# The opening of a two-layer diffusion block: modulation by eighths, products by k tile, written out in order

## The chip, the cores and the metric

One core of a Trainium2 chip runs the whole program. The metric is device microseconds of one execution. TensorE multiplies, ScalarE (ACT) and VectorE (DVE) do the rest, GpSimd (POOL) takes small powers, SyncE (SP) issues nearly all DMA.

## What is computed

Two layers of a hybrid block on 256 latent tokens and 256 context tokens of 1024 channels. Each layer modulates its norms with shifts, gains and gates that come from a condition vector through a large matrix:

```python
m = (silu(c) @ w_ada + b_ada).reshape(1, 1, 9, 1024)        # and mc, from c_ctx
def pre(t, mm, i, gi):  return rms_norm(t, g[gi]) * (1 + mm[:, :, i + 1]) + mm[:, :, i]
def post(t, y, mm, i, gi, wres):  return t + wres * mm[:, :, i + 2] * rms_norm(y, g[gi])
h = post(h, swiglu(pre(h, m, 0, 0), ffn_wi[0], ffn_wo[0]), m, 0, 1, 0.5)   # and hc, with mc
# then attention, a windowed attention, a short convolution; then a second swiglu
def swiglu(u, wi, wo):  g, up = split(u @ wi, 2);  return (silu(g) * up) @ wo
```

All data are float32. The first thing that needs TensorE at length is the first `u @ wi`: 512 tokens, 1024 channels in 8 k tiles, 2816 hidden columns in 22 column tiles, with a gate half and an up half each.

## The kernel before, in words

Token tiles of 128 tokens are H[0] to H[3] (0, 1 latent, 2, 3 context). A float32 product is done as three products of a rounded format: each operand is split into a rounded upper half (ScalarE casts, line 93 for weights into `w[:, 0]`, line 263 for activations into `Uh`) and a remainder (VectorE subtracts, lines 94 and 264, `w[:, 1]` and `Ul`). For one column tile f, one half u and one k tile, three matmuls of 128x512 go into one PSUM bank: upper weight by `Uh`, upper weight by `Ul`, remainder weight by `Uh` (lines 305 to 307). A column tile has 48 of them.

The opening is `pre_first` (line 246) and the first `up_all([0, 1, 2], "k")` of `ffn`. `pre_first` takes the token tiles in the order 2, 3, 0, 1: `normed_t` (line 217) squares both halves on ScalarE, POOL takes the power -1/2, ScalarE scales the tile into `xn`, TensorE turns it by 8 transposes, and ScalarE copies the result to `XT` (line 251). Then come four quarters of the modulation, `ada_quarter` (line 126): 2 MB of `w_ada` in four loads (tiles `adas`), 32 float32 matmuls with the condition as 32-column weights `S`, four of them side by side (line 135), a copy to `grow` (line 138), a transpose (line 140), and VectorE makes the shift `COLS` and the gain `GP` (lines 118 and 122) for two k tiles. `uf` is `XT` scaled and shifted (line 261), and is split into `Uh` and `Ul`. With mode "k", the products of column tiles 0, 1 and 2 go quarter by quarter, two k tiles at a time, in six PSUM banks of the tags `at`, `mm` and `pv`.

Loads go through one queue on SP, in program order. `stg` has two buffers, and a weight load waits until the earlier weight in its buffer is split. The order of the instructions on each engine is set by a scheduler that simulates the program; the kernel's text gives priorities and dependencies. The modulation of all later parts is done on VectorE between other work (`ada_step`, line 147) and is not touched.

## Time and profile before

| | us |
|---|---|
| median of 3 runs | 1709.74 |
| lowest, highest | 1707.21, 1710.19 |
| profiled execution | 1709.25 |
| its span, first to last instruction | 1707.5 |
| TensorE busy in the span | 1677.3 (98%) |
| VectorE, ScalarE, POOL busy | 1148.4, 720.0, 51.1 |
| granted clock, mean | 0.996 |

The time of an execution is its span and a little around it, here 1.75 us. A busy TensorE in the profile is not one at its peak, since the ends of matmuls are modelled; the start of one matmul after the next is the better measure. A granted clock of 1.00 is 2.4 GHz, 0.50 is 1.2 GHz.

### The profile page before, as it was taken

To read this page: it belongs to the slowest core of one execution; us is meant where nothing else is said; L and a number is where in the kernel's file an instruction comes from. 1 tells how busy PE (TensorE), PEld (TensorE's weight loads), DVE (VectorE), ACT (ScalarE), POOL (GpSimd) and SP (SyncE) were. 2 spreads that over 40 slices of the span, in tenths; PEclk is the share of its full clock that TensorE was granted. 3 is DMA by queue.
4 is the path that set the end of the run, shared out by engine and by line. 5 is a ranking of instruction groups with operands and counts; after the bars stand their busy time and mean duration, and the time that the engine had idled before them with its cause. 6 is when DMAs were issued, how large, how long until landed. Compare 5 with 4: busy or idle time off the path is not lost.

```text
span 1707.5 us, 23320 instructions
## 1 busy us (share of the span) xinstructions
PE 1677.3 (98%) x9012; PEld 1412.0 (83%) x9012; DVE 1148.4 (67%) x1915; ACT 720.0 (42%) x1246; POOL 51.1 (3%) x76
## 2 busy tenths in 40 slices
PE   6999999999999999999999999999999999989997
PEld 4888888888877788888888888888888888779997
DVE  3578788667766665475676557778775768766654
ACT  5432222227656583322222364322222657765442
POOL 1000000002000010000000010000000110000000
PEclk9999999999999999999999999999999999999999
DMA  8566555423121234454444235665563323346551
GB/s 316 206 226 200 172 196 197 161 87 112 62 81 43 93 124 160 148 198 150 156 162 136 75 123 186 209 197 197 172 197 113 114 78 118 118 162 219 176 196 63
DMA packets 75567, 260.38 MB, mean 152 GB/s; under 512 B 10536, under 2 KB 13824, under 8 KB 74560
## 3 DMA queue, kind: packets, MB, share of 16 engines
q1 hardware_dynamic: 74256, 253.34, 44.1%
q0 software_dynamic: 1200, 5.55, 0.9%
q8 instruction: 71, 1.16, 0.3%
q14 instruction: 40, 0.33, 0.1%
HBM read 257.76 MB, written 1.09 MB: 152 GB/s over the span
## 4 chain that ended last, share of the span: by engine, by line
PE 96%; DMA 1%; DVE 1%; ACT 1%; issue 0%; SPq 0%; DVEq 0%; POOLq 0%; ACTq 0%
PE mm L79 51%; PE at L79 27%; PE pv L79 15%; PE ptr L581 2%; PE ptr L225 1%; DMA GT<-in_qkg_dram 1%; ACT junk L208 0%; DVE w L94 0%; DMA H<-in_xin_dram 0%; DMA stg<-in_wi_tm_dram 0%; DVE H L271 0%; PE ptr L462 0%; PE ptr L377 0%; ACT xn L220 0%; ACT XT L251 0%
## 5 line engine op out<-in xcount | busy, mean ns | idle before, releaser
L79 PE MATMUL mm<-Uh,w 128*128 128x512 f32 (+1 forms) x1808 | 486.7, 348 | 0.0
L93 ACT CAST w<-stg 128x1024 fp32r<-128x1024 f32 x262 | 274.5, 1050 | 440.4 <-PE mm L79 396.7
L94 DVE TENSOR_TENSOR w<-stg,w 128x1024 fp32r<-128x1024 f32 x262 | 319.7, 1222 | 164.6 <-ACT w L93 163.9
L79 PEld LDWEIGHTS mm<-Uh,w 128*128 128x128 f32 x1808 | 318.7, 189 | 43.5 <-issue 1.9
L79 PE MATMUL mm<-Ul,w 128*128 128x512 f32 (+1 forms) x904 | 314.9, 348 | 0.0
L162 DVE CUSTOM_DVE_ANT_0 uf<-adas,CB 128x1024 f32<-128x1024 f32 x248 | 302.9, 1221 | 17.6 <-DMA adas<-in_w_ada_dram 13.6
L79 PE MATMUL at<-Uh,w 128*128 128x512 f32 (+1 forms) x960 | 253.9, 344 | 0.3 <-ACT Uh L263 0.3
L79 PE MATMUL mm<-w,a 128*128 128x512 f32 x924 | 226.7, 389 | 0.0
L79 PEld LDWEIGHTS mm<-w,a 128*128 128x128 f32 x924 | 173.4, 188 | 35.8
L79 PEld LDWEIGHTS mm<-Ul,w 128*128 128x128 f32 x904 | 171.1, 189 | 21.5 <-issue 0.5
L79 PEld LDWEIGHTS at<-Uh,w 128*128 128x128 f32 x960 | 168.9, 190 | 22.2 <-ACT Uh L263 0.5
L79 PE MATMUL mm<-w,Uh 128*128 128x512 f32 (+1 forms) x544 | 171.8, 388 | 0.0
L79 PE MATMUL at<-Ul,w 128*128 128x512 f32 (+1 forms) x480 | 165.4, 344 | 1.0 <-DVE Ul L264 1.0
L79 PE MATMUL at<-w,a 128*128 128x512 f32 x594 | 146.7, 390 | 0.1
L79 PEld LDWEIGHTS at<-w,a 128*128 128x128 f32 x594 | 111.0, 188 | 23.4 <-ACT a L316 1.0
L79 PE MATMUL pv<-Uh,w 128*128 128x512 f32 (+1 forms) x464 | 127.7, 353 | 0.0
L79 PEld LDWEIGHTS mm<-w,Uh 128*128 128x128 f32 x544 | 100.4, 188 | 19.8 <-issue 0.7
L311 DVE TENSOR_TENSOR sg<-mm,sg 128x512 f32<-128x512 f32 (+1 forms) x86 | 51.3, 597 | 89.5 <-PE mm L79 83.5
L94 DVE TENSOR_TENSOR w<-stgx,w 128x1024 fp32r<-128x1024 f32 x58 | 71.0, 1224 | 53.1 <-ACT w L93 52.9
L79 PE MATMUL mm<-w,Ul 128*128 128x512 f32 (+1 forms) x272 | 105.3, 387 | 0.8 <-DVE Ul L244 0.8
L79 PEld LDWEIGHTS at<-Ul,w 128*128 128x128 f32 x480 | 91.2, 190 | 12.5 <-DVE Ul L264 1.6
L79 PEld LDWEIGHTS pv<-Uh,w 128*128 128x128 f32 x464 | 82.7, 189 | 12.0
(159 smaller groups left out, 1734.3 us busy)
## 6 DMA issues: line engine op xcount, KB each, us to landing
adas<-in_w_ada_dram SPq DMA_DIRECT2D x144, 512.0 KB, 3.7
stg<-in_wi_dram SPq DMA_DIRECT2D x124, 512.0 KB, 4.2
stg<-in_wo_dram SPq DMA_DIRECT2D x66, 512.0 KB, 3.3
stg<-in_win_dram SPq DMA_DIRECT2D x40, 512.0 KB, 3.3
stgx<-in_wi_dram SPq DMA_DIRECT2D x36, 512.0 KB, 4.3
stgx<-in_wo_dram SPq DMA_DIRECT2D x22, 512.0 KB, 4.2
stg<-in_woa_dram SPq DMA_DIRECT2D x16, 512.0 KB, 3.3
stg<-in_wi_tm_dram SPq DMA_DIRECT2D x16, 512.0 KB, 3.4
```

What stands on the lines that cost most here:

```text
L79: pe.matmul(out, lhsT=lhsT, rhs=rhs, start=first, stop=last)
L93: act.copy(w[:, 0], s)
L94: dve.tensor_tensor(out=w[:, 1], in0=s, in1=w[:, 0].bitcast(F32), op=ALU.subtract)
L162: dve.tensor_tensor_reduce(out=junk, in0=s, in1=CB[:, v], op0=ALU.mult, op1=ALU.add, scale=1.0, scalar=0.0, accum_out=ada_mc[m][:, v, cb:c ...
L225: pe.transpose(pt[:, b], xn[:, 128 * k:128 * k + 128], I)
L311: dve.tensor_tensor(out=sg[:, 0:n], in0=pss[f, 1][:, 0:n], in1=sg[:, 0:n], op=ALU.mult)
L581: pe.transpose(pt[:, b], P[:, 128 * b:128 * b + 128], I)
```

## The change

The function `ada_quarter` goes, and `pre_first` is rewritten. It now also loads the weights of the first three column tiles, splits them, does their products and gives back the six filled banks, and `ffn` takes them as `first`. `in_order` chains all instructions traced under it, on each engine, in the order in which they are written, in place of the scheduler's.

The modulation comes in eighths, one k tile each: two loads of 512 KB (`load_ada`), 16 matmuls (`ada_mm`), a copy to `R`, and one matmul of `R` by a small selection matrix `SELM` (`ada_sel`), which replaces the transpose and adds the two halves of the sum. The layout of `w_ada0` in memory follows. The weights of column tiles 0, 1 and 2 are loaded between the first eighths (`load_w`), tile 1 into two buffers of its own.

Token tiles are no longer scaled and transposed: the rsqrt is put on a diagonal (`diag`), and `flip` multiplies the tile by it. Half of the squares and half of the copies go to VectorE (`square`, `keep`). `unit` makes one k tile of `Uh` and `Ul`, the latent half on ScalarE, the context half on VectorE. Ahead of all this TensorE does 16 products of a constant tile (`spin`).

```diff
+    cur, last_of = {}, {}
+
+    @contextmanager
+    def in_order():
+        traced = nc.cur_bb.bb.instructions
+        n0 = len(traced)
+        yield
+        last_of.clear()
+        for ins in traced[n0:]:
+            if ins.engine in last_of:
+                tc.add_manual_dep(ins, last_of[ins.engine].name,
+                                  mybir.DependencyInfo(mybir.DependencyClass.NoSync, mybir.DependencyReason.DATA),
+                                  reason="traced order")
+            last_of[ins.engine] = ins
...
-    def ada_quarter(ph, qd):
...
 
     def pre_first(ph):
         U = new_u()
+        WU = ph.tile([128, 512], F32R, name="WU", tag="WU")
+        dve.memset(WU.bitcast(F32), 1.0)
         XT = ph.tile([128, 8, 512], F32, name="XT", tag="XT")
...
+        SELM = ph.tile([128, 2, 2], F32, name="SELM", tag="SELM")
+        for m in range(2):
+            dve.tensor_reduce(out=SELM[:, m], in_=I[:, 64 * m:64 * m + 64].rearrange("p (q r) -> p r q", q=2)[:, 0:2],
+                              op=ALU.add, axis=AX.X)
+        dummy = ps_tr.tile([128, 4, 128], F32, name="ptr", tag="ptr").rearrange("p b c -> p (b c)")
+
+        def spin(n):
+            for _ in range(n):
+                mm(dummy, WU[:, 0:128], WU, True, True)
+
+        pts, rs, dgs = {}, {}, {}
+
+        def square(t):
+            s0 = sumsq(H[t][:, 0:512], 512)
+            s1 = small.tile([128, 1], F32, name="s1", tag="s1")
+            sq = ph.tile([128, 512], F32, name="sq", tag="sq")
+            dve.tensor_tensor_reduce(out=sq, in0=H[t][:, 512:1024], in1=H[t][:, 512:1024], op0=ALU.mult, op1=ALU.add,
+                                     scale=1.0, scalar=0.0, accum_out=s1)
+            rs[t] = rsum(sum_eps(s0, s1))
+
+        def diag(t):
+            dgs[t] = ph.tile([128, 128], F32, name="dg", tag="dg", bufs=2)
+            act.activation(dgs[t], I, AF.Copy, scale=rs[t])
+
+        def flip(t, hbs=(0, 1)):
+            for hb in hbs:
+                pt = cur["mm"]().rearrange("p (b c) -> p b c", b=4)
+                for b in range(4):
+                    k = 4 * hb + b
+                    mm(pt[:, b], H[t][:, 128 * k:128 * k + 128], dgs[t], True, True)
+                pts[t, hb] = pt
+
+        def keep(t, hb):
+            xt = XT[:, 4 * hb:4 * hb + 4, 128 * t:128 * t + 128]
+            if hb == 0:
+                act.copy(xt, pts[t, 0])
+            else:
+                dve.tensor_copy(out=xt, in_=pts[t, 1])
+
+        psa, ws, pss, Rs = {}, {}, {}, {}
+
+        def load_ada(j):
+            psa[j] = []
+            for h in range(2):
+                s = ph.tile([128, 4, 2, 128], F32, name="adas", tag="adas", bufs=6)
+                sp.dma_start(out=s.rearrange("p a b c -> p (a b c)"), in_=w_ada0[j, h])
+                psa[j].append(s)
+
+        def ada_mm(j):
+            p = ps_tr.tile([128, 4, 128], F32, name="ptr", tag="ptr")[:, 0]
+            ss = psa.pop(j)
+            for kt in range(8):
+                for m in range(2):
+                    g = 2 * m + kt % 2
+                    mm(p[32 * g:32 * g + 32], S[:, kt], ss[kt // 4][:, kt % 4, m], kt < 2, kt >= 6)
+            R = ph.tile([128, 128], F32, name="R", tag="R", bufs=2)
+            act.copy(R, p)
+            Rs[j] = R
+
+        def ada_sel(j):
+            pt = ps_tr.tile([128, 4, 128], F32, name="ptr", tag="ptr")
+            mm(pt[:, 0, 0:4], Rs.pop(j), SELM.rearrange("p m v -> p (m v)"), True, True)
+            for m in range(2):
+                set_cols(m, j, 1, pt[:, 0, 2 * m:2 * m + 2].unsqueeze(1))
+
+        def unit(j):
+            tag = "uf" if j % 2 == 0 else "xn"
+            uf = work.tile([128, 1024], F32, name=tag, tag=tag)
+            for v in range(2):
+                c = slice(256 * v, 256 * v + 256)
+                g, sh = GP[0][:, j, v:v + 1], COLS[0][:, j, v:v + 1]
+                if v == 0:
+                    act.activation(uf[:, c], XT[:, j, c], AF.Identity, scale=g, bias=sh)
+                else:
+                    dve.tensor_scalar(out=uf[:, c], in0=XT[:, j, c], scalar1=g, scalar2=sh, op0=ALU.mult, op1=ALU.add)
+            act.copy(U[0][:, j], uf[:, 0:512])
+            dve.tensor_tensor(out=U[1][:, j], in0=uf[:, 0:512], in1=U[0][:, j].bitcast(F32), op=ALU.subtract)
+
+        stage = {}
+
+        def load_w(f):
+            for u in range(2):
+                if f == 1:
+                    stage[f, u] = ph.tile([128, 1024], F32, name="stgx", tag="stgx", bufs=2)
+                else:
+                    stage[f, u] = stg.tile([128, 1024], F32, name="stg", tag="stg")
+                sp.dma_start(out=stage[f, u], in_=wi[0, 0, f, u])
+
+        def split_w(f, u):
+            s = stage.pop((f, u))
+            w = next_slot()
+            act.copy(w[:, 0], s)
+            dve.tensor_tensor(out=w[:, 1], in0=s, in1=w[:, 0].bitcast(F32), op=ALU.subtract)
+            ws[f, u] = w
+
+        def prod(f, us, j0, j1):
+            for u in us:
+                if (f, u) not in pss:
+                    pss[f, u] = cur["mm"]()
+                for kt in range(j0, j1):
+                    wh, wl = (ws[f, u][:, x, 128 * kt:128 * kt + 128] for x in range(2))
+                    mm(pss[f, u], wh, U[0][:, kt], kt == 0, False)
+                    mm(pss[f, u], wh, U[1][:, kt], False, False)
+                    mm(pss[f, u], wl, U[0][:, kt], False, kt == 7)
+
+        B = (0, 1)
+        with in_order():
+            load_ada(0)
+            load_w(0)
+            load_ada(1)
+            load_w(1)
+            load_ada(2)
+            spin(16)
+            square(2)
+            square(3)
+            diag(2)
+            flip(2)
+            square(0)
+            diag(3)
+            flip(3)
+            keep(2, 0)
+            keep(2, 1)
+            square(1)
+            diag(0)
+            flip(0)
+            keep(3, 0)
+            keep(3, 1)
+            diag(1)
+            keep(0, 0)
+            keep(0, 1)
+            ada_mm(0)
+            flip(1, (0,))
+            ada_sel(0)
+            keep(1, 0)
+            flip(1, (1,))
+            unit(0)
+            keep(1, 1)
+            split_w(0, 0)
+            split_w(0, 1)
+            load_w(2)
+            load_ada(3)
+            prod(0, B, 0, 1)
+            ada_mm(1)
+            ada_sel(1)
+            load_ada(4)
+            unit(1)
+            split_w(1, 0)
+            split_w(1, 1)
+            prod(0, B, 1, 2)
+            prod(1, (0,), 0, 2)
+            ada_mm(2)
+            prod(1, (1,), 0, 2)
+            ada_sel(2)
+            load_ada(5)
+            unit(2)
+            split_w(2, 0)
+            split_w(2, 1)
+            prod(0, B, 2, 3)
+            prod(1, B, 2, 3)
+            ada_mm(3)
+            load_ada(6)
+            prod(2, (0,), 0, 1)
+            ada_sel(3)
+            unit(3)
+            prod(2, (0,), 1, 3)
+            prod(2, (1,), 0, 3)
+            for j in range(3, 8):
+                if j < 7:
+                    ada_mm(j + 1)
+                if j == 3:
+                    load_ada(7)
+                prod(0, B, j, j + 1)
+                if j < 7:
+                    ada_sel(j + 1)
+                    unit(j + 1)
+                prod(1, B, j, j + 1)
+                prod(2, B, j, j + 1)
+        return U, pss
...
-    def ffn(ph, l, i, U, tiles, after, ada_target, mode):
+    def ffn(ph, l, i, U, tiles, after, ada_target, mode, first=None):
...
             pss = {(f, u): cur["mm"]() for f in fs for u in range(2)}
+            up_mm(fs, ws, pss, segs, c0)
+            up_out(fs, pss, c0, n)
+
+        def up_mm(fs, ws, pss, segs, c0):
...
+
+        def up_out(fs, pss, c0, n):
...
         def up_all(fs, mode=""):
-            if mode == "k":
-                segs = [(2 * qd, 2, lo_c, n_c) for qd in range(4)]
-            elif mode[0:3] == "tok":
+            if mode[0:3] == "tok":
                 segs = [(0, 8, 256, 256), (0, 8, 0, 256)]
...
-            up_all([0, 1, 2], mode)
-            up_all([3])
+            if mode == "k":
+                with ExitStack() as behind:
+                    for ins in last_of.values():
+                        behind.enter_context(tc.issue_after(ins))
+                    up_out([0, 1, 2], first, lo_c, n_c)
+                    up_all([3])
+            else:
+                up_all([0, 1, 2], mode)
+                up_all([3])
...
     with phase("st") as ph:
-        U = pre_first(ph)
+        U, first = pre_first(ph)
...
-        ffn(ph, 0, 0, U, order, after, 54, "k")
+        ffn(ph, 0, 0, U, order, after, 54, "k", first)
...
-    first = a["w_ada"][0, :, 0:2048].reshape(4, 2, 128, 2, 4, 256)
-    arrays["w_ada0"] = first.transpose(4, 0, 2, 1, 3, 5).reshape(4, 4, 128, 1024)
+    first = a["w_ada"][0, :, 0:2048].reshape(2, 4, 128, 2, 8, 128)
+    arrays["w_ada0"] = first.transpose(4, 0, 2, 1, 3, 5).reshape(8, 2, 128, 1024)
```

How the instructions move on TensorE, at the beginning (`adas` modulation loads, `dg` the diagonal, `WU` the constant tile, `R` and `grow` the modulation before it is turned). Before:

```order
L225 MATMUL ptr<-I,xn 128x128 x8
L79 MATMUL at<-adas,S 32x128 x8
L225 MATMUL ptr<-I,xn 128x128 x8
L79 MATMUL at<-adas,S 32x128 x24
L225 MATMUL ptr<-I,xn 128x128 x8
L79 MATMUL mm<-adas,S 32x128 x16
L225 MATMUL ptr<-I,xn 128x128 x8
L79 MATMUL mm<-adas,S 32x128 x8
L140 MATMUL ptr<-I,grow 128x128
L79 MATMUL mm<-adas,S 32x128 x8
L140 MATMUL ptr<-I,grow 128x128
L79 MATMUL at<-adas,S 32x128 x8
```

Now:

```order
L92 MATMUL ptr<-WU 128x512 x16
L92 MATMUL at<-dg,H_84 128x128 x4
L92 MATMUL mm<-dg,H_84 128x128 x4
L92 MATMUL at<-dg,H_85 128x128 x4
L92 MATMUL mm<-dg,H_85 128x128 x4
L92 MATMUL pv<-dg,H_82 128x128 x4
L92 MATMUL mm<-dg,H_82 128x128 x4
L92 MATMUL ptr<-adas,S 32x128 x16
L92 MATMUL at<-dg,H_83 128x128 x4
L92 MATMUL ptr<-SELM,R 128x4
L92 MATMUL mm<-dg,H_83 128x128 x4
L92 MATMUL at<-Uh,w 128x512
```

Before, the turns and the modulation of a quarter and a half stand ahead of the first product; now the constant products, all turns by the diagonal and one eighth do, and the selection stands within the last turn.

TensorE around the second and third k tile. Before:

```order
L79 MATMUL at<-Uh,w 128x512
L79 MATMUL at<-Ul,w 128x512
L79 MATMUL at<-Uh,w 128x512 x2
L79 MATMUL at<-Ul,w 128x512
L79 MATMUL at<-Uh,w 128x512
L79 MATMUL at<-adas,S 32x128 x24
L79 MATMUL at<-Uh,w 128x512
L79 MATMUL at<-Ul,w 128x512
L79 MATMUL at<-Uh,w 128x512 x2
L79 MATMUL mm<-adas,S 32x128 x8
L79 MATMUL mm<-Uh,w 128x512
```

Now:

```order
L92 MATMUL mm<-Uh,w 128x512
L92 MATMUL mm<-Ul,w 128x512
L92 MATMUL mm<-Uh,w 128x512
L92 MATMUL ptr<-adas,S 32x128 x16
L92 MATMUL ptr<-SELM,R 128x4
L92 MATMUL at<-Uh,w 128x512
L92 MATMUL at<-Ul,w 128x512
L92 MATMUL at<-Uh,w 128x512
L92 MATMUL mm<-Uh,w 128x512
L92 MATMUL mm<-Ul,w 128x512
L92 MATMUL mm<-Uh,w 128x512
L92 MATMUL pv<-Uh,w 128x512
```

Before, six products are followed by three loads' worth of modulation of the next quarter and by more products; now a whole eighth and its selection stand directly ahead of the products that use them.

The queue on SP, from the token tiles on. Before:

```order
L681 DMA H_84<-in_xin_dram 128x1024
L681 DMA H_85<-in_xin_dram 128x1024
L681 DMA H_82<-in_xin_dram 128x1024
L681 DMA H_83<-in_xin_dram 128x1024
L131 DMA adas<-in_w_ada_dram 128x1024 x8
L91 DMA stg<-in_wi_dram 128x1024 x2
L131 DMA adas<-in_w_ada_dram 128x1024 x8
L91 DMA stg<-in_wi_dram 128x1024 x4
L151 DMA CB<-in_crow_dram 128x2048
```

Now:

```order
L849 DMA H_84<-in_xin_dram 128x1024
L849 DMA H_85<-in_xin_dram 128x1024
L849 DMA H_82<-in_xin_dram 128x1024
L849 DMA H_83<-in_xin_dram 128x1024
L290 DMA adas<-in_w_ada_dram 128x1024 x2
L331 DMA stg<-in_wi_dram 128x1024 x2
L290 DMA adas<-in_w_ada_dram 128x1024 x2
L331 DMA stgx<-in_wi_dram 128x1024 x2
L290 DMA adas<-in_w_ada_dram 128x1024 x2
L331 DMA stg<-in_wi_dram 128x1024 x2
L290 DMA adas<-in_w_ada_dram 128x1024 x10
L104 DMA stg<-in_wi_dram 128x1024 x2
```

The same loads of token tiles come first; then two loads of modulation and two of weights take turns, where eight and two did.

## Rows read from the trace of the kernel before

**Rows 1.** The page: chain of work that ended last, by engine.

```profile
PE 96%; DMA 1%; DVE 1%; ACT 1%; issue 0%; SPq 0%; DVEq 0%; POOLq 0%; ACTq 0%
```

**Rows 2.** TensorE timeline (start, busy us, line, operation, tiles, count); chain piece (start, us).

```profile
67.26 0.39 PE L79 MATMUL at<-Uh,w 128*128 128x512 f32 x1
...
66.06 1.36 PE mm L79 x6
```

**Rows 3.** Timeline of TensorE, 9 to 31 us; in brackets idle before and releaser.

```profile
18.47 1.09 PE L225 MATMUL ptr<-I,xn 128*128 128x128 f32 x8
19.49 1.08 PE L79 MATMUL mm<-adas,S 128*32 128x128 f32 x32
...
22.36 0.64 PE L79 MATMUL mm<-adas,S 128*32 128x128 f32 x16
...
25.43 0.64 PE L79 MATMUL at<-adas,S 128*32 128x128 f32 x16 [0.83 <-DMA adas<-in_w_ada_dram]
26.35 0.49 PE L79 MATMUL at<-Uh,w 128*128 128x512 f32 x1 [0.27 <-ACT Uh L263]
27.89 0.50 PE L79 MATMUL at<-Ul,w 128*128 128x512 f32 x1 [1.04 <-DVE Ul L264]
28.22 0.89 PE L79 MATMUL at<-Uh,w 128*128 128x512 f32 x2
```

**Rows 4.** Windows: length, busy us (count) of PE, PEld, DVE, ACT, POOL; clock; DMA.

```profile
21.58:25.00 3.42, 2.58 (x42) 1.64 (x40) 1.56 (x7) 2.12 (x4) 0.00 (x0) 1.00 1.01 405
25.00:28.41 3.41, 1.66 (x19) 1.04 (x20) 3.38 (x7) 2.16 (x3) 0.00 (x0) 1.00 1.02 408
28.41:31.82 3.41, 3.41 (x40) 2.42 (x43) 2.30 (x6) 1.04 (x1) 0.00 (x0) 0.50 1.04 414
```

**Rows 5.** DMA: rate in 40 slices of 1 us; the H tiles' issue and landing.

```profile
GB/s 0 7 96 224 362 421 397 404 414 397 401 422 418 397 401 426 410 401 401 426 414 397 397 418 406 406 410 418 406 406 410 418 406 410 332 57 16 0 0 37
...
1.65 1.93 SPq L681 DMA_DIRECT2D H<-in_xin_dram  x4
...
DMA to landing us min/median/max: 4.3/6.0/7.4
```

**Rows 6.** Timeline of ScalarE, 5 to 31 us.

```profile
6.00 0.63 ACT L208 ACTIVATE junk<-H 128x512 bf16<-128x512 f32 x1 [2.02 <-DMA H<-in_xin_dram]
6.54 0.19 ACT L208 ACTIVATION_READ_ACCUMULATOR junk<-H 128x1 f32 x1
...
12.87 1.15 ACT L220 ACTIVATE xn<-H,rr 128x1024 f32<-128x1024 f32 x1
...
22.02 1.07 ACT L251 COPY XT<-ptr 128x512 f32<-128x512 f32 x2 [0.75 <-PE ptr L225]
23.95 0.27 ACT L138 COPY grow<-mm 128x128 f32<-128x128 f32 x1 [0.86 <-PE mm L79]
24.12 1.05 ACT L93 CAST w<-stg 128x1024 fp32r<-128x1024 f32 x1
```

**Rows 7.** Timeline of TensorE, 31 to 37 us.

```profile
32.99 0.63 PE L79 MATMUL at<-Uh,w 128*128 128x512 f32 x2
33.55 0.64 PE L79 MATMUL mm<-adas,S 128*32 128x128 f32 x16
34.12 0.50 PE L79 MATMUL mm<-Uh,w 128*128 128x512 f32 x1
```

**Rows 8.** Timeline of VectorE, 5 to 31 us.

```profile
23.30 0.23 DVE L118 TENSOR_TENSOR COLS<-ptr,BC 128x4 f32<-128x4 f32 x2 [8.42 <-PE ptr L140]
...
23.83 1.38 DVE L261 TENSOR_SCALAR uf<-XT,GP,COLS 128x256 f32<-128x256 f32 x4
```

**Rows 9.** Groups of instructions, shapes apart: count, busy us, mean ns, idle before.

```profile
L317 DVE TENSOR_TENSOR a<-sg,a 128x512 fp32r<-128x512 f32 x56 | 38.3, 684 | 0.7 <-ACT a L316 0.7
L316 ACT CAST a<-sg 128x512 fp32r<-128x512 f32 x56 | 34.6, 618 | 9.2 <-DVE sg L311 8.6
...
L239 ACT ACTIVATE uf<-ptr,COLS,GP 128x128 f32<-128x128 f32 x72 | 27.0, 457 | 13.2 <-PE ptr L225 11.3 <-DVE Ul L244 1.8
```

More of the change, by code (lines that the diff above doesn't have):

```diff
@@ L59, in tile_hybrid_block @@
     pool.dma_start(out=CW, in_=convw)
-    dve.tensor_scalar(out=GC, in0=GC, scalar1=32.0, scalar2=None, op0=ALU.mult)
     dve.memset(S, 0.0)
@@ L63, in tile_hybrid_block @@
     dve.memset(NHALF, -0.5)
+    dve.tensor_scalar(out=GC, in0=GC, scalar1=32.0, scalar2=None, op0=ALU.mult)
     act.activation(S[:, :, 0:2], C2, AF.Silu)
-    cur = {}
+    cur, last_of = {}, {}
[11 more added lines that the diff above has]
+            last_of[ins.engine] = ins
     def bank(tag):
@@ L124, in set_cols @@
                 in1=GC[:, gi, k0:k0 + nk].unsqueeze(2).to_broadcast([128, nk, 2]), op0=ALU.add, op1=ALU.mult)
-    def ada_quarter(ph, qd):
-        pb = cur["mm"]()
-        p = pb[:, 0:128]
-        for kp in range(4):
-            s = ph.tile([128, 2, 2, 256], F32, name="adas", tag="adas", bufs=8)
-            sp.dma_start(out=s.rearrange("p a b c -> p (a b c)"), in_=w_ada0[qd, kp])
-            for k2 in range(2):
-                kt = 2 * kp + k2
-                for j in range(4):
-                    mm(p[32 * j:32 * j + 32], S[:, kt], s[:, k2, j // 2, 128 * (j % 2):128 * (j % 2) + 128],
-                       kt == 0, kt == 7)
-        R = work.tile([128, 2, 512], F32, name="grow", tag="grow")[:, 0]
-        act.copy(R[:, 0:128], p)
-        pt = ps_tr.tile([128, 4, 128], F32, name="ptr", tag="ptr")
-        pe.transpose(pt[:, 0], R[:, 0:128], I)
-        pv = pt[:, 0].rearrange("p (m q r) -> p m q r", m=2, q=2)
-        for m in range(2):
-            set_cols(m, 2 * qd, 2, pv[:, m, :, 0:2])
     ada_cb, ada_mc = {}, {}
@@ L247, in pre_first @@
         U = new_u()
+        WU = ph.tile([128, 512], F32R, name="WU", tag="WU")
+        dve.memset(WU.bitcast(F32), 1.0)
         XT = ph.tile([128, 8, 512], F32, name="XT", tag="XT")
-        for t in (2, 3, 0, 1):
-            for hb, pt in normed_t(t):
-                act.copy(XT[:, 4 * hb:4 * hb + 4, 128 * t:128 * t + 128], pt)
-        for qd in range(4):
-            ada_quarter(ph, qd)
-            uf = work.tile([128, 8, 128], F32, name="uf", tag="uf")
-            uv = uf.rearrange("p (k c) t -> p k (c t)", k=2)
-            ks = slice(2 * qd, 2 * qd + 2)
-            for k2 in range(2):
-                k = 2 * qd + k2
-                for v in range(2):
-                    c = slice(256 * v, 256 * v + 256)
-                    dve.tensor_scalar(out=uv[:, k2, c], in0=XT[:, k, c], scalar1=GP[0][:, k, v:v + 1],
-                                      scalar2=COLS[0][:, k, v:v + 1], op0=ALU.mult, op1=ALU.add)
-            act.copy(U[0][:, ks], uv)
-            dve.tensor_tensor(out=U[1][:, ks], in0=uv, in1=U[0][:, ks].bitcast(F32), op=ALU.subtract)
@@ L265, in pre_first @@
-        return U
+        SELM = ph.tile([128, 2, 2], F32, name="SELM", tag="SELM")
[7 more added lines that the diff above has]
+        pts, rs, dgs = {}, {}, {}
```

## The prediction

> **What bounds the kernel now.** I read the chain of waits first: TensorE holds 96% of it [rows 1], so time can only be won where TensorE waits, and that is the opening. There the mark I use is the end of the first three column tiles of the feed-forward part (144 products of 128x512): the fourth tile's first product starts at 67.26 [rows 2]. From then on TensorE is busy throughout, in the same work before and after the change, so whatever moves this mark moves the end by as much. Six products take 1.36 us, 0.2267 each, so the 144 are 32.65 us. They start at 26.35 [rows 3]; 67.26 - 26.35 leaves 40.9, so 8.3 us go to other things: seven of the sixteen modulation loads and two transposes that stand among the products, waits of 1.0 and 0.3, and a clock at 1.2 GHz from 28.41 to 31.82 [rows 4], where two products take 0.89 [rows 3] instead of 0.63 [rows 7].
>
> Before 26.35 there are two supplies. DMA moves 400 to 420 GB/s from 4 us on, and the last token tile lands about 10.5 (the four issues end at 1.65 + 1.93, the longest takes 7.4) [rows 5]; a load of 512 KB then lands every 1.28 us. ScalarE squares, scales and copies all four tiles: two squares of 0.63 + 0.19, a scaling of 1.15 and two copies, 1.07 together, until the copies at 22.02 are done [rows 6]. Only then comes the first modulation turn.
>
> **What a matmul of float32 costs.** It is the term that decides, and it is hidden in the counts. A token tile is turned by 8 transposes, and they are 8 records in the trace, 1.09 us at full clock. The modulation matmuls are two records each: where the program has 8, the trace has 16 (four at a time on 32 columns). 16 records last 0.64 and 32 last 1.08, so 16 more are 0.44 [rows 3]. Between products, 16 records cost 0.67: a pair starts at 32.99, its second ends at 33.45, the next product starts at 34.12 [rows 7].
>
> **The change, term by term.**
>
> *Arrivals.* The token tiles come first as before. The first eighth is 1 MB instead of 2: it is complete at 10.5 + 2 x 1.28 = 13.0, the weights of tile 0 at 15.6, the second eighth at 18.2, tile 1 at 20.7. Later loads come at the same pace, and all eighths together are the same 8 MB. In my sum none of them is waited for again: the third eighth would be there at 23.3 and is wanted at 29. SP's later loads wait for a freed buffer, but land at least 2 us ahead of use; the weights of the fourth tile are split some 2 us before its start.
>
> *Token tiles.* ScalarE loses one square, the scaling and one copy per tile (to VectorE, or to a 128x128 scaling that I take at 0.27, a 128-wide copy [rows 6]). The price is that a turn by the diagonal is a true float32 product: two records a block, 16 a tile, 1.75 us at 0.11 a record instead of 1.09. This is beside the loads, but it stands ahead of the modulation on TensorE: turns of tile 0 until 13.8, first eighth until 14.9, half a tile's turn, selection at 15.8.
>
> *First product.* From selection: 0.4 to its result, 0.53 for shift and gain (23.30 to 23.83 [rows 8]), 0.59 for a scaled and shifted 128x256 on ScalarE (0.46 for 128 columns, and 0.11 for 128 more, a quarter of what a rounding of 1024 takes over one of 512), 0.62 for the rounding [rows 6, 9], hops of 0.05: rounded at 18.0. The first weight is rounded behind it on ScalarE, 1.05 less the overlap, so the first product starts at 18.9, 7.4 us earlier than now. The 16 products on a constant run from 1.9 to about 8 and delay nothing.
>
> *What is among the products from there.* 32.65 for the 144. Now seven whole eighths stand there, 16 matmuls or 32 records each, 0.67 + 0.44 = 1.11: 7.8 us (before, seven runs of 16 records, 4.7). Seven selections of two records, 0.2: 1.4 us.
>
> *Waits that the new order makes.* TensorE runs what is written, in order. The lower halves of the first two weights come off VectorE at 20.5 and 21.65, behind the remainder of the first unit and a copy: 1.1 + 0.5. Then the second eighth, its copy on ScalarE (0.5), its selection, and products that need the unit made from it: from selection to its rounded half 0.4 + 0.53 + 0.59 + 0.62 + hops = 2.2, of which 2.0 are idle, and 0.5 more for its remainder (0.69 [rows 9]). The third eighth does the same, 2.0 + 0.5, since nothing stands between its selection and the products that need it. Together 7.1. From the fourth on, 12 products and the next eighth (3.8) cover the 2.9 of that chain, and I cost nothing more; were that cover gone, it would be up to 2 us a turn, five times.
>
> Sum at full clock: 18.9 + 32.65 + 7.8 + 1.4 + 7.1 = 67.9, against 67.26 now. The head start of 7.4 is eaten by 3.1 + 1.2 of matmuls that used to run while TensorE had nothing else to do, and by waits of 7.1 where there are now 1.3 and the slow clock.
>
> *The clock.* Now it fell to 1.2 GHz at 28.41; from 25.00 to there TensorE had 16 modulation records and three products, busy for 1.66 us by the profile, with gaps of 0.83 and 1.04 [rows 3, 4]. In my sum TensorE has even less to do between 17 and 20 (two products) and between 23 and 26 (a selection and one or two). So I expect a fall to 1.2 GHz there in spite of the early warm-up, and the dense run from 26.5 on to begin at that clock. The stretch at 1.2 GHz in the trace lasts 3.41; if all of such a stretch held dense work it would cost 1.7, two of them 3.4. Lower bound 0, upper bound 4.3 (two stretches and part of the gaps); I take 2.5, nearest to the row but with more than one stretch likely.
>
> The Trainium skill (TensorE: Matmul & The Clock Gate, "Why this matters for your kernels") puts a fall of the clock down to one long idle gap between bursts of matmuls, longer than any in my sum. By that rule the clock would stay up and this term would be 0. The trace disagrees: the clock fell after gaps of 1 us at the most.
>
> *What the sum misses.* The same working on the opening of before, with its order and landings, gives 66.9 where the trace has 67.26. I add 0.3. So 70.7, later by 3.4. The profiled execution took 1709.25, 0.5 under the median of the runs (1709.74), so the changed kernel is put at 1709.25 + 3.4 = **1712.7 us**.
>
> **Rivals.**
>
> *The clock holds* (the 16 products and the turns, now true products, keep it up): 67.9 + 0.3 = 68.2, 0.9 later, 1710.2. For it: after 21.58 to 25.00, with TensorE busy for 2.58 of 3.42, the clock stayed up [rows 4]. Against it: the emptier stretches above.
>
> *Faster than before.* The mechanism: the two bare turns at the second and third eighth overlap better than I sum them (ScalarE's and VectorE's 256-column halves together, the remainder under the first products), or turns by the diagonal cost one record and not two. One record a block lets the first product start about 2 earlier; 2 us less in the waits and the clock up as well: 68.2 - 4 = 64.2, 3 earlier, 1706.2. It decides from the point where the first product starts before 18 and the gaps after it sum to under 5. Against it stands the count of records.
>
> *Slower still*: the clock stays at 1.2 GHz over two stretches and the thin turn of the third eighth brings it down a second time. Dense work in half clock from 25 to 32 and some of 36 to 40 puts the mark at 72.5: 5.3 later, 1714.5.
>
> **How the numbers follow.** About 0.2% (3.4 us) is what a measurement of this kernel can tell from no change; the forecast sits at its edge. Chances: the forecast with one stretch or a little more at half clock 0.43, the clock holds 0.2, slower still 0.22, faster 0.15. Of the forecast's own range (1711 to 1714.4) two fifths are slower by over 0.2% of the median (1713.2), of the slower rival nearly all: 0.38. Faster by over 0.2% (under 1706.3) is about the faster rival: 0.16. The rest, 0.46, is within 0.2%. The range runs from the clock-holds case with an error of 3 us in my waits, 1707.2, to the slower rival with 1 us of error, 1715.5; outside are the faster rival and the last of the slower.
>
> **What would show it.** In the trace of the changed kernel: first product of 128x512 at 19 (17 or under: the turns are cheap); 256 modulation records, 32 in a run, seven runs after the first product; idle of about 2 us ahead of the products of the second and third k tile, put down to the rounded half; granted clock 0.5 in a stretch between 20 and 32; the fourth tile's first product at 70 to 71. A mark before 66 makes the forecast wrong, and so does a clock that never falls after 9 us; a mark after 73 means that the turns from the fourth eighth on are not covered.

## The result, and the profile after

The changed kernel takes 1727.65 us (median of 4 runs, 1726.07 to 1728.47) against 1709.97 (4 runs, 1707.21 to 1711.98): a ratio of 1.0103, 95% interval [1.0091, 1.0115]. It is slower by 17.7 us, 12 us past the end of the range. The profiled execution took 1728.47, 19.2 more than the profiled one of before. In the experiments below the kernel before was timed beside each run; its medians there lie between 1710.74 and 1710.90.

The opening comes first. TensorE's timeline of the changed kernel (start, busy us, line, operation, tiles, count, idle before and releaser):

```profile
13.94 1.08 PE L92 MATMUL ptr<-adas,S 128*32 128x128 f32 x32
14.95 1.16 PE L92 MATMUL at<-dg,H 128*128 128x128 f32 x8
...
19.03 0.50 PE L92 MATMUL at<-Uh,w 128*128 128x512 f32 x1 [1.80 <-ACT w L336]
...
22.55 1.94 PE L92 MATMUL ptr<-adas,S 128*32 128x128 f32 x32
24.87 0.59 PE L92 MATMUL ptr<-SELM,R 128*128 128x4 f32 x2 [0.39 <-ACT R L301]
27.25 0.80 PE L92 MATMUL at<-Uh,w 128*128 128x512 f32 x1 [1.80 <-ACT Uh L320]
...
52.44 1.08 PE L92 MATMUL ptr<-adas,S 128*32 128x128 f32 x32
54.95 0.28 PE L92 MATMUL ptr<-SELM,R 128*128 128x4 f32 x2
58.01 1.08 PE L92 MATMUL ptr<-adas,S 128*32 128x128 f32 x32
...
73.14 0.39 PE L92 MATMUL at<-Uh,w 128*128 128x512 f32 x1
```

The first product starts at 19.03 instead of 26.35 [rows 3], an eighth is 32 records, and the bare turn of 1.80 ahead of the second eighth's products stands where the forecast had 2.0. The fourth column tile's first product, the mark, is at 73.14 against 67.26 [rows 2]: 5.9 later, where 3.4 was forecast. The windows of the same kernel, cut where the granted clock changes (length, busy us and count of PE, PEld, DVE, ACT, POOL, clock, DMA), answer to [rows 4]:

```profile
12.82:19.86 7.04, 5.13 (x63) 4.19 (x61) 3.42 (x9) 4.82 (x8) 0.00 (x0) 1.00 1.03 417
19.86:33.51 13.65, 10.78 (x62) 7.26 (x66) 5.62 (x9) 3.44 (x6) 0.00 (x0) 0.50 0.75 293
33.51:73.14 39.63, 37.60 (x326) 29.36 (x319) 14.51 (x36) 15.61 (x25) 0.00 (x0) 1.00 0.46 175
```

The stretch at 0.50, which is 1.2 GHz, lasts 13.65 us; before, it lasted 3.41.

That leaves 13.3 us of the profiled executions' 19.2 which are lost after the mark, where nothing was to change. The chain of waits gives no hint: TensorE holds 97% of it, and after the mark it waits 6.5 us where it waited 6.7 before. The groups of instructions do (count, busy us, mean ns of one, idle before). These are the down products, which stream the weights `w` past the activations `a`, after the change and then before:

```profile
L92 PE MATMUL mm<-w,a 128*128 128x512 f32 x924 | 232.0, 395 | 0.0
...
L92 PE MATMUL at<-w,a 128*128 128x512 f32 x594 | 149.9, 395 | 0.1
```

```profile
L79 PE MATMUL mm<-w,a 128*128 128x512 f32 x924 | 226.7, 389 | 0.0
```

The same 924 took 389 ns each before and take 395 now. These times overlap; what counts is the distance between starts, and the timeline shows it: 12 products take from 105.79 to 108.58, 232.5 ns each, where a product of before takes 226.7 (an up product by [rows 2], a down product by its trace between 100 and 370 us).

```profile
105.79 2.95 PE L92 MATMUL at<-w,a 128*128 128x512 f32 x12
108.58 2.95 PE L92 MATMUL mm<-w,a 128*128 128x512 f32 x12
```

There are 924 + 594 + 330 = 1848 of them, spread over the whole kernel: 1848 x 5.7 ns = 10.5 us of the 13.3. The up products, in which `Uh` streams past `w`, kept theirs (227).

### The profile page after: what moved, and what is told of

It is laid out like the page before. It is cut to its first block, busy times and chain, and to the rows that moved or that the text cites. A ratio compares the mean times of both kernels' runs of the same rounds, so it can differ in the third digit from the quotient of the medians.

```text
span 1726.7 us, 23489 instructions
## 1 busy us (share of the span) xinstructions
PE 1702.0 (99%) x9072; PEld 1424.1 (82%) x9072; DVE 1154.1 (67%) x1938; ACT 718.0 (42%) x1250; POOL 47.8 (3%) x76
## 3 DMA queue, kind: packets, MB, share of 16 engines
q8 instruction: 71, 1.16, 0.3%
HBM read 257.76 MB, written 1.09 MB: 150 GB/s over the span
## 4 chain that ended last, share of the span: by engine, by line
PE 97%; DVE 1%; DMA 1%; ACT 1%; issue 0%; SPq 0%; POOL 0%; DVEq 0%; POOLq 0%; ACTq 0%
PE mm L92 51%; PE at L92 27%; PE pv L92 15%; PE ptr L749 2%; PE ptr L219 1%; PE ptr L92 1%; DMA stg<-in_wi_tm_dram 0%; DMA H<-in_xin_dram 0%; DVE w L107 0%; ACT w L106 0%; DMA stg<-in_win_dram 0%; DVE H L428 0%; PE ptr L630 0%; PE ptr L538 0%; ACT Uh L320 0%
## 5 line engine op out<-in xcount | busy, mean ns | idle before, releaser
L106 ACT CAST w<-stg 128x1024 fp32r<-128x1024 f32 x256 | 267.8, 1049 | 450.2 <-PE mm L92 396.4
L107 DVE TENSOR_TENSOR w<-stg,w 128x1024 fp32r<-128x1024 f32 x256 | 312.4, 1222 | 154.4 <-ACT w L106 153.4
L92 PE MATMUL mm<-w,a 128*128 128x512 f32 x924 | 232.0, 395 | 0.0
```

The lines of the kernel that those rows point to most:

```text
L92: pe.matmul(out, lhsT=lhsT, rhs=rhs, start=first, stop=last)
L106: act.copy(w[:, 0], s)
L107: dve.tensor_tensor(out=w[:, 1], in0=s, in1=w[:, 0].bitcast(F32), op=ALU.subtract)
```

## The experiments: the place of a tile

What differs for the down products? Not their order. But the change takes a new tag in the pool `small`: `s1`, four buffers of 4 bytes which the allocator puts 32 bytes apart. So every pool behind `small` starts 128 bytes higher, the `a` tiles among them; `w`, `Uh` and `Ul`, allocated ahead of it, did not move. Added up from the tile sizes in the kernel's text, what lies between `w` and `a` was a multiple of 256 bytes before, and is 128 more after. Theory P says that this place is the cause, its rival O that something in the new order is.

**The changed kernel with `a` moved back.**

```diff
-            s1 = small.tile([128, 1], F32, name="s1", tag="s1")
+            s1 = small.tile([128, 1], F32, name="s1", tag="ss", bufs=12)
```

> The changed kernel with one edit: the sum of squares that VectorE leaves in `square` takes a buffer of the tag `ss` instead of the new tag `s1`, so that every pool of the phases behind the opening starts 128 bytes lower, where it started before the change. No instruction moves. Theory P (place): the down products, which read their stationary operand from `a`, go from 232.5 back to 226.8 ns start to start, some 1850 of them, and with them about 10 to 13 us of the time go: 1715 to 1717 us, which leaves about 6 us for the opening. Rival O (order): they are slow because of what runs beside them in the new order; then 1727 us, unchanged.

1717.51 us (4 runs), ratio 1.0038 [1.0023, 1.0053]: 10.1 us of the 17.7 are gone. Its groups and timeline show the old rate (109.04 - 106.32 = 2.72 for 12, 226.7 ns):

```profile
L92 PE MATMUL mm<-w,a 128*128 128x512 f32 x924 | 226.8, 390 | 0.0
```

```profile
106.32 2.88 PE L92 MATMUL at<-w,a 128*128 128x512 f32 x12
109.04 2.88 PE L92 MATMUL mm<-w,a 128*128 128x512 f32 x12
```

**The kernel before with the same shift.**

```diff
+    PAD = small.tile([128, 32], F32, name="pad", tag="pad", bufs=1)
+    dve.memset(PAD, 0.0)
```

> The kernel before with one edit: an unused tile of 128 bytes a partition in the pool `small`, so that the pools of the phases start 128 bytes higher, where they start in the changed kernel. Theory P: the down products take 232.5 ns instead of 226.8, and the time is 10 to 13 us longer, 1720 to 1723 us. Rival O: no change, 1709.7 us within 0.2%.

1721.45 us, ratio 1.0062 [1.0045, 1.0079]: a tile that nobody reads costs 10.6 us, and the group's row is the changed kernel's:

```profile
L81 PE MATMUL mm<-w,a 128*128 128x512 f32 x924 | 232.0, 395 | 0.0
```

Rival O is out on both sides.

**Everything 32 bytes higher.**

```diff
+    PAD = const.tile([128, 8], F32, name="PAD")
+    dve.memset(PAD, 0.0)
```

> The kernel before with an unused tile of 32 bytes at the start of the pool `const`: every tile behind it, weights, Uh, Ul and a alike, lies 32 bytes higher, and their distances stay. If the place of one operand alone decides (its start in some block of memory), products of some kinds leave 226.8 ns in one direction or the other, by up to 6 ns (13 us over 1850 products, 45 us if all 7500 move). If only the distance between the stationary and the moving operand decides, nothing moves: 226.8 ns everywhere and 1709.7 us.

1710.44 us in one run (the kernel before, timed beside it: 1710.87), and the down products start every 226.8 ns (the mean of some 460 distances between 100 and 370 us). So it is not the place of one operand that decides, but how the two lie to each other.

**The measurement by itself.** One kernel, no other work, one execution: 16 stationary tiles at the multiples of 32 bytes within 512, 16 moving tiles likewise, each pair multiplied 24 times (`LETTERS` are A to P, `s` stationary, `m` moving).

```diff
+    # stationary tiles: 1056 bytes apart, so each starts 32 bytes further in its 512; moving tiles: 2080 bytes apart
+    s = [const.tile([128, 264], F32R, name=f"s{c}") for c in LETTERS]
+    m = [const.tile([128, 520], F32R, name=f"m{c}") for c in LETTERS]
...
+            for k in range(24):
+                o = 128 * (k % 2)
+                pe.matmul(p, lhsT=s[j][:, o:o + 128], rhs=m[i][:, 0:512], start=k == 0, stop=k == 23)
```

> No part of the reference is computed here: a measurement by itself. 16 stationary tiles that start at the 16 multiples of 32 bytes within 512, and 16 moving tiles likewise; each pair is multiplied 24 times (128 rows, 128x512, float32r), two stationary slices in turn, nothing else running. Theory P: the distance from start to start depends on the place of the stationary or moving tile alone, with nothing beside it: 226.7 ns for some pairs (stationary at 96 of 512, moving at 352, as before the change) and 232.5 ns for others (stationary at 224). Rival O: 226.7 ns for all 256 pairs, since nothing runs beside the products.

TensorE's timeline of this kernel, for one moving tile; a letter further is 32 bytes further, and tiles of one letter start alike within 256 bytes, as do letters 8 apart:

```profile
986.76 5.76 PE L35 MATMUL p<-mL,sA 128*128 128x512 f32 x24
992.36 5.66 PE L35 MATMUL p<-mL,sB 128*128 128x512 f32 x24
...
1003.45 5.61 PE L35 MATMUL p<-mL,sD 128*128 128x512 f32 x24
1008.89 5.75 PE L35 MATMUL p<-mL,sE 128*128 128x512 f32 x24
...
1025.69 5.76 PE L35 MATMUL p<-mL,sH 128*128 128x512 f32 x24
...
1036.90 5.67 PE L35 MATMUL p<-mL,sJ 128*128 128x512 f32 x24
...
1048.00 5.61 PE L35 MATMUL p<-mL,sL 128*128 128x512 f32 x24
```

`sD` and `sL` are the fast ones, `sB` and `sJ` next, the rest alike: (1008.89 - 1003.45) / 24 = 226.7 ns against (992.36 - 986.76) / 24 = 233.3. Over all 256 pairs the distance between starts goes by one number, the stationary start less the moving start, modulo 256 bytes:

| stationary - moving, mod 256 | 0 | 32 | 64 | 96 | 128 | 160 | 192 | 224 |
|---|---|---|---|---|---|---|---|---|
| mean ns from start to start (32 pairs each, without the very first) | 226.8 | 233.1 | 233.4 | 233.9 | 233.4 | 233.4 | 229.3 | 233.4 |

Pairs of one column differ by 1.4 ns at most; the very first pair, 291 ns in the mean, is left out. In the kernel before, `w`, `Uh`, `Ul` and `a` all start alike within 256 bytes, the one fast distance; the change put `a` at a distance of 128. There the kernel has 232.5 ns and the table 233.4; these 0.9 ns are not explained. What I had written down for theory P, that the place of one operand alone decides, does not hold: the distance of the two decides. Why the chip does this, no run here shows.

## The experiments: the opening

With `a` back, 6.6 us are left (1717.51 against 1710.87), with the mark at 73.68 in that run's profile, 6.4 after the 67.26 of before. All runs from here have `a` in its old place.

**Spare products in the waits.**

```diff
+        def hold(n):
+            for fu in ((0, 0), (0, 1), (1, 0), (1, 1), (2, 0)):
+                if fu not in pss:
+                    pss[fu] = cur["mm"]()
+            for _ in range(n):
+                mm(pss[2, 0], WU[:, 0:128], WU, True, True)
...
             load_ada(3)
-            prod(0, B, 0, 1)
+            hold(7)
+            prod(0, (0,), 0, 1)
+            hold(3)
+            prod(0, (1,), 0, 1)
             ada_mm(1)
+            hold(1)
             ada_sel(1)
...
+            hold(8)
             prod(0, B, 1, 2)
...
             ada_sel(2)
+            hold(8)
```

> The changed kernel with its pools back in place (as the run that moved `a` back, 1717.5 us, the mark of the fourth column tile's first product at 73.7 us), and in the waits of the opening 27 spare products of WU by WU into the bank of the third tile, which its first real product clears: 7 ahead of the first products, 3 between the first two, 1 ahead of the second selection, 8 ahead of each of the second and the third eighth's products. Theory C (clock): the 13.65 us at a granted clock of 0.50 (from 20.4 to 34.1 us) are what the opening costs beyond the forecast of 70.7: with the waits filled the clock stays at 1.00, the mark comes at 69 to 70 us and the time at 1713 to 1714 us. Rival W (waits): the mark hangs on when ScalarE and VectorE bring the operands and the slower clock only fills those waits; then 73 to 74 us and 1717 to 1718 us, or later by what the spare products hold up.

1712.71 us (10 runs), ratio 1.0011 [1.0002, 1.0021]: 4.8 us come back by adding 27 products that compute nothing. The same window in the kernel with `a` back, and in this one:

```profile
20.41:34.07 13.66, 10.70 (x59) 7.12 (x62) 5.81 (x9) 3.63 (x6) 0.00 (x0) 0.50 0.77 291
```

```profile
20.41:34.07 13.66, 12.95 (x109) 9.61 (x110) 6.22 (x13) 4.61 (x8) 0.00 (x0) 1.00 0.95 348
```

And the timeline of this one; the spare products fill the bare turn, so that no wait is left ahead of 26.36, and the mark moves from 73.68 to 69.65:

```profile
24.41 2.08 PE L92 MATMUL at<-WU 128*128 128x512 f32 x8
26.36 0.50 PE L92 MATMUL at<-Uh,w 128*128 128x512 f32 x1
...
69.65 0.39 PE L92 MATMUL at<-Uh,w 128*128 128x512 f32 x1
```

So theory C holds: the slow stretch cost 3.6 us between first product and mark (73.68 - 19.77 against 69.65 - 19.38).

**Without the 16 products at the start.**

```diff
-            spin(16)
```

> The changed kernel with its pools back in place, without the 16 spare products at the start (`spin(16)`). Theory S: they keep the turns fast; without them the records of the turns and of the first eighth run at about twice their 0.11 us until some 18 us, 3.5 us for a tile instead of 1.75, the fourth tile is turned 2 to 4 us later, and first product, mark and time come 1 to 4 us later (1718.5 to 1721.5 us). Rival A (arrivals): the turns wait for tiles, squares and diagonals anyway, so the first product moves by under 1 us; and if TensorE's clock then rises later, it may not be at 0.50 when the products begin, as before the change (low for 3.41 us only): the mark up to 4 us earlier, down to 1713.5 us.

1719.79 us (4 runs), ratio 1.0053 [1.0036, 1.007]: 2.3 slower, of which the size is not sharp, since the intervals of the two ratios overlap. The first turns run slow, 0.21 us a record and not 0.11; the first product starts at 21.18, 1.4 later than with them, the mark is at 75.52, 1.8 later, and the clock still falls afterwards (0.50 in three stretches between 23 and 43 us). Theory S holds in these three numbers. But the slow records end at 12.7 us, not at 18. The trace's first record of the granted clock begins there too, so the 1.00 that a windows row gives for the time before it has nothing behind it.

```profile
8.56 2.08 PE L92 MATMUL at<-dg,H 128*128 128x128 f32 x8 [8.56 <-ACT dg L267]
10.43 1.91 PE L92 MATMUL mm<-dg,H 128*128 128x128 f32 x8
12.13 1.34 PE L92 MATMUL at<-dg,H 128*128 128x128 f32 x8
13.31 1.06 PE L92 MATMUL mm<-dg,H 128*128 128x128 f32 x8
...
21.18 0.50 PE L92 MATMUL at<-Uh,w 128*128 128x512 f32 x1 [1.81 <-ACT w L336]
```

**Transposes in place of the diagonal.**

```diff
-            dgs[t] = ph.tile([128, 128], F32, name="dg", tag="dg", bufs=2)
-            act.activation(dgs[t], I, AF.Copy, scale=rs[t])
+            tag = "xn" if t % 2 == 0 else "uf"
+            dgs[t] = work.tile([128, 1024], F32, name=tag, tag=tag)
+            act.activation(dgs[t], H[t], AF.Copy, scale=rs[t])
...
-                    mm(pt[:, b], H[t][:, 128 * k:128 * k + 128], dgs[t], True, True)
+                    pe.transpose(pt[:, b], dgs[t][:, 128 * k:128 * k + 128], I)
```

> The changed kernel with its pools back in place, in which a tile is scaled by ScalarE as a whole (1.15 us, as before the change) and turned by transposes against the identity, instead of being multiplied by a diagonal that ScalarE makes in 0.27 us. Theory D: the diagonal saves ScalarE 4 times 0.88 = 3.5 us in its queue ahead of the casts of the first weights, so that the first product comes 2 to 3.5 us later without it and the time is 1718 to 1721 us. Rival: the first product waits for the last arrivals and the casts are late for another reason; then it moves by under 1 us and the time is 1717 to 1718 us.

1716.49 us (5 runs), ratio 1.0032 [1.0019, 1.0045]: not slower than with the diagonal, and the first product starts at 18.97, 0.8 earlier. Theory D falls: ScalarE's 3.5 us did not stand on the path. With the diagonal ScalarE waits 0.80 for POOL, then 1.35 and 0.79 for TensorE, ahead of the first cast at 18.68; without it the cast starts at 17.88. The edit also shortens the turns on TensorE, so what each half of it does alone is not shown. Half a tile is turned in 0.66 us and not 1.16, one record a block:

```profile
15.30 0.66 PE L275 MATMUL at<-I,uf 128*128 128x128 f32 x4
...
18.97 0.50 PE L92 MATMUL at<-Uh,w 128*128 128x512 f32 x1 [2.34 <-ACT w L337]
```

**The kernel before with the 16 products alone.**

```diff
+        dummy = ps_tr.tile([128, 4, 128], F32, name="ptr", tag="ptr").rearrange("p b c -> p (b c)")
+        for _ in range(16):
+            mm(dummy, WU[:, 0:128], WU, True, True)
```

> The kernel before with one part of the change alone: the 16 spare products of WU by WU at the start. Its transposes at 10.10 and 14.08 us (1.97 us for 8) run in 1.09, its first 64 records of the modulation in half the time. Theory A (arrivals): its first product at 26.35 us waits for the last modulation weights, so the mark stays at 67 to 68 us and the time within 0.2% of 1710 us. Rival C: an early high clock falls later, as in the changed kernel: a stretch at 0.50 of 7 to 14 us among the first products, the mark 2 to 4 us later, 1712 to 1714 us.

1710.79 us (10 runs), ratio 1.0001 [0.9991, 1.001]: theory A, no change. Its transposes do run in 1.09, its first product is at 26.14 and its mark at 67.63; its clock was at 0.50 for 6.83 us from 26.6, as rival C had it, and that cost nothing that the time shows.

**Another order.** Does the opening need its bare turns? Here each eighth is multiplied and selected a step earlier; the diff is against the kernel with `a` back, and in one of two runs five spare products stand ahead of `ada_mm(1)` (3) and `ada_mm(2)` (2).

```diff
             ada_mm(0)
+            load_ada(3)
...
             split_w(0, 0)
-            split_w(0, 1)
-            load_w(2)
-            load_ada(3)
-            prod(0, B, 0, 1)
             ada_mm(1)
-            ada_sel(1)
             load_ada(4)
+            ada_sel(1)
+            split_w(0, 1)
+            load_w(2)
             unit(1)
+            prod(0, B, 0, 1)
             split_w(1, 0)
             split_w(1, 1)
             prod(0, B, 1, 2)
-            prod(1, (0,), 0, 2)
             ada_mm(2)
-            prod(1, (1,), 0, 2)
-            ada_sel(2)
             load_ada(5)
+            prod(1, (0,), 0, 2)
+            ada_sel(2)
             unit(2)
...
+            prod(1, (1,), 0, 2)
             ada_mm(3)
...
+            prod(2, (0,), 0, 4)
+            prod(2, (1,), 0, 4)
```

> The kernel of the run f1_hold with another order of the same work: each eighth is multiplied and selected one step earlier (the second while the first weights are cast, the third and fourth among the products of the second and third), the loads of the fourth and fifth eighth are issued ahead of the third tile's weights, that tile's products come after four k tiles, and spare products stand at two places (3 and 2) instead of four. Theory: the two bare turns of 1.8 us ahead of the second and third eighth's products (and 0.78 and 0.23 beside them) come from the order, not from arrivals; with them gone the mark moves from 69.65 to 62 to 65 us, ahead of the 67.26 of the kernel before, and the time to 1705 to 1708 us. Rival: the arrivals (the third eighth lands at 24.07 us, the third tile's weights at 27.3) take their place, the mark stays at 68 to 70 and the time at 1711 to 1713 us.

> As g1_order_hold without any spare product behind the first 16. Theory: what is left of the waits (0.9 us ahead of the second eighth's multiplication, some of 0.5 us behind) lets the granted clock fall to 0.50 for 3.41 us or more, at a cost of 0.5 to 4 us of the time against g1_order_hold. Rival: with the bare turns gone TensorE is busy enough and the clock stays; within 0.5 us of g1_order_hold.

With five spare products: 1711.29 us, ratio 1.0002 [0.9993, 1.0011], mark 66.72. Without any: 1709.96, ratio 0.9995 [0.9985, 1.0004], mark 64.06 (10 runs each). The order was the cause of the waits: 64.06 is 3.2 ahead of the kernel before, and 7.6 us of the time come back against the 1717.51 of the old order. The forecast times of 1705 to 1708 us were missed by both, and the first of the two marks as well. What I expected of the spare products did not come: in the profile with them the clock fell for 6.83 us from 22.3, in the one without it stayed up. One profile shows one execution: this one, without spare products, took 1708.80 at a mean granted clock of 0.996, and seven of the ten had 0.993 or 0.994, so in most the clock was at 0.50 for longer, at a place that is not recorded.

```profile
22.30:29.10 6.80, 6.45 (x42) 3.92 (x41) 3.13 (x4) 2.51 (x3) 0.00 (x0) 0.50 1.03 412
```

```profile
22.30:29.10 6.80, 6.04 (x52) 4.26 (x52) 3.89 (x8) 3.38 (x5) 0.00 (x0) 1.00 1.03 409
```

The 3.2 at the mark are still 3.0 at 1500 us, and 0.6 at the end. They are given back where the last feed-forward block starts. There the kernel before waits 2.81 and 1.95, behind its transposes at 1503.53:

```profile
1503.53 1.04 PE L225 MATMUL ptr<-I,xn 128*128 128x128 f32 x8
1507.37 0.50 PE L79 MATMUL at<-w,Uh 128*128 128x512 f32 x1 [2.81 <-ACT Uh L243]
1510.04 0.79 PE L79 MATMUL at<-w,Ul 128*128 128x512 f32 x1 [1.95 <-DVE Ul L244]
...
1517.56 1.03 PE L225 MATMUL ptr<-I,xn 128*128 128x128 f32 x8
```

The kernel without spare products has the same transposes 3.0 earlier and the next ones 0.6 earlier:

```profile
1500.51 1.04 PE L219 MATMUL ptr<-I,xn 128*128 128x128 f32 x8
1505.49 0.79 PE L92 MATMUL at<-w,Uh 128*128 128x512 f32 x1 [3.94 <-ACT Uh L237]
1506.08 0.63 PE L92 MATMUL mm<-w,Uh 128*128 128x512 f32 x1
1508.16 0.79 PE L92 MATMUL at<-w,Ul 128*128 128x512 f32 x1 [1.45 <-DVE Ul L238]
...
1516.98 1.03 PE L219 MATMUL ptr<-I,xn 128*128 128x128 f32 x8
```

From the transposes to the first product it takes 4.98 instead of 3.84, and from there to the next transposes 11.49 instead of 10.19, with the clock at 0.50 for 10.24 us instead of 3.41. On ScalarE a weight cast that waited 1.02 for its load stands ahead of the awaited `Uh`; in the kernel before the same cast does not wait:

```profile
1503.87 1.04 ACT L106 CAST w<-stg 128x1024 fp32r<-128x1024 f32 x1 [1.02 <-DMA stg<-in_wi_tm_dram]
1504.83 1.13 ACT L237 CAST Uh<-uf 128x512 fp32r<-128x512 f32 x2
```

**The same place with spare products**, in that kernel and, as a control, in the one before.

```diff
...
+            if len(tiles) == 2:
+                spare = bank("pv")
+                with tc.issue_after(first_turn[0].ins):
+                    for _ in range(24):
+                        mm(spare, wt[0][0][:, 0, 0:128], wt[0][0][:, 0, 0:512], True, True)
             for t in tiles:
                 c = slice(128 * t, 128 * t + 128)
                 p = [tm_block(U, t, wt[u]) for u in range(2)]
...
```

> The kernel of the run g2_order_bare (mark at 64.06 us, 3.2 us ahead of the kernel before, of which its end kept 0.6) with 24 spare products behind the transposes of the first token tile at the start of the last feed-forward block, where TensorE waits 3.94 and 1.45 us for the operands and the granted clock then stood at 0.50 for 10.24 us. Theory: the opening's gain is given back there, 1.1 us in a late load and 1.3 us in the clock; with the clock held the end keeps 2 to 4 us against the kernel before, 1706.5 to 1709 us. Rival: the wait for the operands sets the time there and the clock only fills it; 1710 us, as without.

> The control: the kernel before with the same 24 spare products at the same place, where its granted clock stood at 0.50 for 3.41 us. Theory: 0 to 1.5 us faster than 1710.8 us, so that g3_order_tail stays 2 to 3 us ahead of it by its opening alone. Rival: as much faster as g3_order_tail is against g2_order_bare, and the two kernels level.

1707.70 us, ratio 0.9984 [0.9975, 0.9993], and 1708.34, ratio 0.9988 [0.9979, 0.9997] (11 runs each). Both are faster than the kernel before, the first by 3.0 us, and it is the fastest of this study. The clock there rose from 0.71 (without spare products) to 1.00, and in the control from 0.89 to 1.00:

```profile
1497.00:1513.20 16.20, 10.81 (x38) 8.08 (x38) 11.38 (x17) 12.14 (x21) 1.70 (x3) 0.71 0.75 251
```

```profile
1497.00:1513.20 16.20, 15.93 (x79) 12.69 (x76) 11.41 (x19) 11.96 (x23) 2.26 (x4) 1.00 0.70 235
```

But the two lie 0.6 apart, within their intervals, not the 2 to 3 us expected: by the times the control's rival, that they are level, holds. Part of it the profile shows: in this execution the clock fell once in the opening (3.41 us from 24.3), with the mark at 65.55 and not 64.06, though the opening is the same code. The control's mark is at 67.14, and of the 1.6 between the two marks 1.6 are left at the end of the same two executions (spans of 1705.5 and 1707.1). So the gain of the new order over the kernel before is not shown by the medians; only its mark is.

## Why the prediction was wrong

- **The step that failed** is the sentence on the mark: that from there on TensorE is busy "in the same work before and after the change, so whatever moves this mark moves the end by as much". The work is the same and its duration is not. The working follows order, queues and waits, and never asks where the change puts the tiles; 10 of the 17.7 us come from four buffers of 4 bytes. Nothing in the prediction, and no rival, has this term. The sentence fails in a second, smaller way too: waits and clock behind the mark do not stay as they were. With `a` back the profiled execution is 8.0 us behind the one of before and its mark 6.4, and near 1515 us its clock was at 0.50 for 6.83 us instead of 3.41; in the other order 3.2 us won at the mark were 0.6 at the end.
- **Arrivals and first product**: right, 19.03 against 18.9. **The turns** are two records a block, as read from the counts; the diagonal takes ScalarE 0.39 and not 0.27.
- **Waits that the new order makes**: right in place and size. With the clock up (the run with spare products) first product to mark is 69.65 - 19.38 = 50.3; less 32.65 of products and 10.4 of eighths, 7.2 are left for waits and what fills them, where the sum had 7.1; how much of that the spare products themselves hold up is not shown. The other order shows that they were a choice and not forced by the loads.
- **Eighths among the products**: mis-sized. I took 1.11 + 0.2 = 1.31 for an eighth and its selection; a full period is 58.01 - 52.44 = 5.57, less 18 products (4.08) leaves 1.49. Seven times 0.18 is 1.3.
- **The clock term**: the direction was right, the size was 2.5 and is 3.6 to 3.8 (19.03 to 73.14 is 54.1, 3.8 more than the 50.3), inside the bounds of 0 to 4.3. The two misses, 1.3 and 1.2, make the 2.4 by which the mark came after 70.7. With them alone the time would have been about 1715, in the range; the run with `a` back, 1717.5, is 2.4 more and just outside it, of which 1.6 are the kernel before itself, 1710.87 beside that run and not the 1709.25 I built on.
- **The clock of before**: I set "the slow clock" against the new waits as a cost of before. With everything 32 bytes higher the clock did not fall there at all, and the mark was at 67.83: the fall had hidden in other waits.
- **The rival "the clock holds"** fell: the clock went to 0.50 at 19.86, and from the first token tile's turns to there no gap on TensorE is longer than the 1.80 us ahead of the first product. The Trainium skill (TensorE: Matmul & The Clock Gate, "Why this matters for your kernels") puts a fall down to one long idle gap between bursts, longer than that; this trace does not agree. Of the rival "slower still" the long stretch came true.
- **What would show it**: the mark came after 73 (73.14), which was to mean turns from the fourth eighth on that are not covered. They are covered: from 39 us on no wait is left, and a period is the sum of its parts.

## What to carry to other kernels

Where a change adds or drops a tile, compare the start addresses of the operands of the big matmuls before and after, and keep stationary and moving tiles at the same place within 256 bytes (shown here for float32r products of 128x512, not for other shapes); the profile shows it as a mean that moves in a group which the change did not touch, here 389 to 395 ns. Compare those groups first, before any story about the code that was edited. Moving independent work ahead of other work on a busy engine wins only if the gaps that the written order makes are filled too: here an order with the same parts took the mark from 73.7 to 64.1 us and the time from 1717.5 to 1710.0, level with the kernel before.

## What was not expected of the hardware

- The rate of float32r products of 128x512 depends on the distance of their two operands in SBUF: 226.8 ns at 0 modulo 256 bytes, 229.3 at 192, 233 to 234 at the six others, with nothing else running. In the kernel a distance of 128 cost 10.1 to 10.6 us.
- TensorE's granted clock fell or stayed in executions of the same opening, on two chips: the mark was at 64.06 in one profile and 65.55 in another.
- A granted clock of 1.00 can mean that nothing is recorded. Without the early products the window row from 8.00 to 18.30 gives 1.00, yet 8 records took 2.08 us at 8.56 and 1.06 from 13.31 on; the trace's first record of the clock begins at 12.7. In the kernel before it begins at 18.2, and there 8 transposes took 1.97 us until then and 1.09 from 18.47 on [rows 3]. Whether TensorE is still slow at its start is to be read from the distance of its records.
